# Shifting where the matmul operands begin in on-chip memory: activations to 0, weights to 64 modulo 256 bytes

## The chip, the cores and the metric

One core of a Trainium2 chip runs one program. The metric is its time on the device in microseconds, median of several runs; each comparison is made on the same chip. TensorE multiplies, VectorE, ScalarE and GpSimd work beside it, and SyncE issues nearly all DMA transfers.

## The reference

One inference step of a two-layer streaming encoder, over 512 new frames of one stream (the prompt) and 16 new frames of each of 8 running streams (the sample), 640 columns of 1024 features in all. Cut to what matters:

```python
def swiglu_ffn(h, g, w_in, w_out):
    a, b = jnp.split(rms_norm(h, g) @ w_in, 2, axis=-1)
    return h + (jax.nn.silu(a) * b) @ w_out

def conv_module(h, hist, ...):
    a, gate = jnp.split(rms_norm(h, g) @ w_pw1 + b_pw1, 2, axis=-1)
    full = jnp.concatenate([hist, a * jax.nn.sigmoid(gate)], axis=1)
    y = depthwise_conv(full, w_dw) + b_dw                    # width 31, causal
    return h + silu(layer_norm(y, ln_g, ln_b)) @ w_pw2 + b_pw2, full[:, -30:]

# layer 0: h = conv_module(h); h = swiglu_ffn(h)
# then   : k, v = split(rms_norm(h, norm_kv) @ w_kv)
# layer 1: q = rms_norm(h, norm_attn) @ w_q; h += band_attention(q, k, v, rel_bias) @ w_o
#          h = swiglu_ffn(h)
# end    : y = rms_norm(h, norm_final)
```

The width is D = 1024, the FFN's hidden width F = 2816 (22 tiles of 128), 16 heads of 64. Everything is float32.

## The kernel before, in words

Features lie on the 128 partitions, frames along the free dimension. The 640 columns are held as two groups, group 0 of 256 columns and group 1 of 384 (`GR`). So a matmul of a weight tile moves either 256 or 384 columns.

**Three products for one.** Precision is kept by splitting every operand into a rounded part and a rest. `wsplit` (L119) loads up to 2048 columns of weights into `raw` (1 MB), ScalarE writes the rounded part `whi` (L141) and VectorE or GpSimd the rest `wlo` (L145); with gains folded in these are L133 and L134. Each of the three tags has two buffers in the pool `wp`. `xsplit` (L149) does the same for activations, at L150 and L151. The normalised activations of a group are kept as `xh` and `xl` (`new_xs`, L153), here called `xs`; the FFN's hidden activations as a pair `hid`. `mm3` (L158) then issues, for each tile of the contraction, three matmuls into one accumulator:

```python
for i, ((wh, wl), (xh, xl)) in enumerate(zip(wts, xs)):
    nc.tensor.matmul(ps, wh, xh, start=(i == 0), stop=False)          # L161
    nc.tensor.matmul(ps, wl, xh, start=False, stop=False)             # L162
    nc.tensor.matmul(ps, wh, xl, start=False, stop=(i == last))       # L163
```

The second argument is stationary (loaded into the array), the third moves through it. In almost all uses the weights are stationary. `proj_v` (L660) is the other way round: there `xs` is stationary and the weights move, 256 columns at a time.

**The stages**, in order: the pointwise layers and the convolution (`pw1`, `conv`, `pw2`; VectorE does most of the convolution at L425) interleaved, by a written plan, with the first part of FFN 0; the rest of FFN 0; attention with its projections (`proj_kq` L638, `proj_v`, `proj_o`, and the heads); FFN 1; the final norm.

**The FFN** (`ffn`, L309) takes the 22 hidden tiles in chunks. For each hidden tile, `ffn_in` (L259) multiplies 2 halves x 8 tiles of the contraction x 3 products, 48 matmuls a group, moving `xs`. Then `ffn_out` (L293) takes the chunk's hidden tiles as contraction and produces 8 output tiles, moving `hid`. In layer 0 group 0 runs alone for 18 hidden tiles in chunks of 6, then both groups for a chunk of 4, then group 1 alone for 18 in chunks of 6. In layer 1 both groups run together, group 1 ahead of group 0 for each hidden tile, in chunks of 9, 9 and 4; an output tile of a 9-chunk is 27 matmuls a group, and group 1 and group 0 alternate. With a chunk of 4, an output tile is 12 matmuls, and the 8 tiles of one group run ahead of the 8 of the other.

**Where buffers begin.** A pool hands out addresses in each partition one after the other, each tile rounded up to 32 bytes. The pool `cst` comes first: the residual stream `h`, small constants, the tile `i4` (L342), then the four tiles `xh`, `xl` of both groups, some more, and as its last tile `t256s` (L579). Then come the weight pool `wp`, and behind it all the other pools, which follow its end. `XPAD` lengthens `i4` and so moves `xs` and all that is behind it; `WPAD` lengthens `t256s` and so moves the weights and all that is behind them. `OPAD` and `HPAD` pad single tiles further on.

Of the kernel before, what the change touches and what calls it, by code (L numbers as in the profile page):

```python
# [54 lines left out]
SSQ = 'avavavav'  # L55
SCUT = 8
CB, QB, KB = 5, 1, 1
XPAD, WPAD, OPAD, HPAD = 24, 8, 16, 16
OG = (0, 1)
BO = "a0 s0 a1 s1 b0 b1 t0 p0 c0 t1 c1"  # L60
BL = "a0 s0 a1 s1 t0 b0 b1 c0 t1 c1 p0"
# [912 lines left out]
```

## Time and profile before

| | |
|---|---|
| time before, median of 3 runs | 1578.71 us (1578.55 to 1582.74) |
| the profiled execution's own time | 1581.78 us |
| its span, first to last instruction | 1580.0 us, mean granted clock 0.983 |
| TensorE matmul busy | 1506.5 us (95%), 10998 matmuls |
| VectorE busy | 970.0 us (61%) |
| ScalarE busy | 604.6 us (38%) |
| GpSimd busy | 398.1 us (25%) |
| DMA | 199.98 MB, mean 127 GB/s |

Lines such as L161 are lines of the kernel; a group of instructions is named by line, engine, operation, and out <- in by the program's tile names with buffer numbers left out (`mm<-xh,whi`: an accumulator from `xh` and `whi`). PE is the matmul, PEld the load of its stationary operand, which overlaps other matmuls. The shown duration of a matmul (280 ns and more) is its passage through the pipeline; a stream of them starts one every 113 to 177 ns, which is read from the start times of the timeline.

### The profile page before, as it was taken

How to read it: one execution, taken by the hardware profiler on the slowest of the kernel's cores; microseconds unless marked ns; L12 is line 12 of the kernel's file. 1: busy time of each engine (PE TensorE's matmuls, PEld its weight loads, DVE VectorE, ACT ScalarE, POOL GpSimd, SP SyncE). 2: the span in 40 equal slices, each digit the busy share in tenths (PEclk: the TensorE clock that was granted, in tenths of full speed). 3: DMA queues.
4: the chain of work that ended last, by engine and by line, in shares of the span. 5: the costliest groups of instructions: out<-in, count | busy, mean ns of one | idle time of the engine just before them, and what ended most of it. 6: DMA issues, size and time to landing. Idle time of an engine off the chain costs nothing.

```text
span 1580.0 us, 26820 instructions
## 1 busy us (share of the span) xinstructions
PE 1506.5 (95%) x10998; PEld 1435.8 (91%) x10998; DVE 970.0 (61%) x1781; ACT 604.6 (38%) x1064; POOL 398.1 (25%) x368
## 2 busy tenths in 40 slices
PE   5988998989999999999999999998999999999997
PEld 5868898889999999999987798886999999999997
DVE  5995999978544555456776668576644334433345
ACT  4544454535433323235654345443422112221222
POOL 6864568867501000004221111011200000000001
PEclk9999999999999999999999999998999999999998
DMA  7884345444412333433655554550221231212311
GB/s 238 237 227 136 123 128 163 138 161 142 150 56 81 121 124 117 147 114 118 234 179 168 177 186 155 162 182 28 81 73 48 66 121 58 77 46 76 107 54 67
DMA packets 58700, 199.98 MB, mean 127 GB/s; under 512 B 10193, under 2 KB 22737, under 8 KB 45777
## 3 DMA queue, kind: packets, MB, share of 16 engines
q1 hardware_dynamic: 58288, 197.96, 38.9%
q8 instruction: 86, 1.41, 0.4%
q10 hardware_dynamic: 288, 0.31, 0.1%
q14 instruction: 38, 0.30, 0.1%
HBM read 187.02 MB, written 11.22 MB: 125 GB/s over the span
## 4 chain that ended last, share of the span: by engine, by line
PE 74%; DVE 15%; DMA 3%; ACT 3%; issue 2%; POOL 2%; SPq 0%; POOLq 0%; ACTq 0%; DVEq 0%
PE mm L161 22%; PE mm L163 22%; PE mm L162 22%; DVE w L425 5%; DVE wlo L145 4%; PE w L780 1%; DMA x<-sc 1%; DVE xl L151 1%; PE am L765 1%; PE am L748 1%; PE am L811 1%; ACT whi L141 1%; DVE hid L151 1%; DMA raw<-in_w_pw 1%; PE w L724 1%
## 5 line engine op out<-in xcount | busy, mean ns | idle before, releaser
L162 PE MATMUL mm<-xh,wlo 128*128 128x256 f32 (+1 forms) x2048 | 636.3, 312 | 14.3 <-DVE wlo L145 13.7
L161 PE MATMUL mm<-xh,whi 128*128 128x256 f32 (+1 forms) x2048 | 632.7, 312 | 7.8 <-ACT xh L150 3.6
L163 PE MATMUL mm<-xl,whi 128*128 128x256 f32 (+1 forms) x2048 | 632.6, 311 | 1.0 <-DVE xl L151 0.9
L162 PEld LDWEIGHTS mm<-xh,wlo 128*128 128x128 f32 x2048 | 390.3, 191 | 17.5 <-DVE wlo L145 16.5
L161 PEld LDWEIGHTS mm<-xh,whi 128*128 128x128 f32 x2048 | 388.2, 191 | 13.0 <-ACT xh L150 6.6
L163 PEld LDWEIGHTS mm<-xl,whi 128*128 128x128 f32 x2048 | 388.6, 190 | 3.5 <-DVE xl L151 2.4
L141 ACT ACTIVATE whi<-raw 128x2048 fp32r<-128x2048 f32 (+3 forms) x140 | 235.0, 1682 | 333.7 <-PE mm L163 278.4
L145 DVE TENSOR_TENSOR wlo<-raw,whi 128x2048 fp32r<-128x2048 f32 (+6 forms) x140 | 262.1, 1874 | 77.8 <-ACT whi L141 77.2
L162 PE MATMUL mm<-hid,wlo 128*128 128x384 f32 (+1 forms) x704 | 216.4, 308 | 6.6 <-DVE wlo L145 6.6
L163 PE MATMUL mm<-hid,whi 128*128 128x384 f32 (+1 forms) x704 | 214.2, 307 | 0.1
L161 PE MATMUL mm<-hid,whi 128*128 128x384 f32 (+1 forms) x704 | 212.8, 307 | 0.0
L145 POOL TENSOR_TENSOR wlo<-raw,whi 128x1536 fp32r<-128x1536 f32 (+3 forms) x50 | 145.3, 2910 | 72.1 <-ACT whi L141 71.5
L280 DVE TENSOR_TENSOR t<-mm,bc 128x384 f32<-128x384 f32 x66 | 33.9, 513 | 188.7 <-PE mm L163 188.7
L162 PEld LDWEIGHTS mm<-hid,wlo 128*128 128x128 f32 x704 | 132.1, 188 | 8.0 <-DVE wlo L145 8.0
L163 PEld LDWEIGHTS mm<-hid,whi 128*128 128x128 f32 x704 | 132.1, 188 | 0.5 <-DVE hid L151 0.3
L161 PEld LDWEIGHTS mm<-hid,whi 128*128 128x128 f32 x704 | 131.2, 188 | 0.2
L218 POOL TENSOR_TENSOR rst<-rst,mhalf 128x2 f32<-128x2 f32 (+1 forms) x7 | 5.9, 849 | 452.5 <-DVE rst L214 452.5
L291 DVE TENSOR_TENSOR h<-mm,h 128x384 f32<-128x384 f32 (+1 forms) x112 | 53.9, 486 | 104.4 <-PE mm L163 104.3
L425 DVE SCALAR_TENSOR_TENSOR w<-gp,dwv,w 128x384 f32<-128x384 f32 x180 | 103.9, 611 | 0.8
L279 ACT ACTIVATE t<-t 128x384 f32<-128x384 f32 x66 | 32.3, 489 | 159.2 <-DVE t L278 159.2
L150 ACT ACTIVATE hid<-t 128x384 fp32r<-128x384 f32 (+1 forms) x88 | 40.5, 461 | 116.9 <-DVE t L281 83.4
L184 POOL TENSOR_TENSOR acc<-sq,sq 128x384 f32<-128x384 f32 (+1 forms) x9 | 9.3, 1028 | 265.0 <-ACT sq L168 264.9
(154 smaller groups left out, 1896.5 us busy)
## 6 DMA issues: line engine op xcount, KB each, us to landing
raw<-in_w_in SPq DMA_DIRECT2D x62, 1024.0 KB
raw<-in_w_pw SPq DMA_DIRECT2D x22, 1024.0 KB
raw<-in_w_out SPq DMA_DIRECT2D x24, 768.0 KB
cache<-in_ck SPq DMA_DIRECT2D x32, 512.0 KB
cache<-in_cv SPq DMA_DIRECT2D x32, 512.0 KB
raw<-in_w_out SPq DMA_DIRECT2D x16, 576.0 KB
raw<-in_w_kq SPq DMA_DIRECT2D x8, 1024.0 KB
x<-sc SPq DMA_DIRECT2D x16, 368.0 KB
```

The lines of the kernel that those rows point to most:

```text
L141: nc.scalar.activation(out=hi[:, a:b], in_=raw[:, a:b], func=AF.Copy)
L145: eng.tensor_tensor(out=lo[:, a:b], in0=raw[:, a:b], in1=hi[:, a:b].bitcast(F32), op=ALU.subtract)
L150: nc.scalar.activation(out=hi, in_=src, func=AF.Copy)
L151: nc.vector.tensor_tensor(out=lo, in0=src, in1=hi.bitcast(F32), op=ALU.subtract)
L161: nc.tensor.matmul(ps, wh, xh, start=(i == 0), stop=False)
L162: nc.tensor.matmul(ps, wl, xh, start=False, stop=False)
L163: nc.tensor.matmul(ps, wh, xl, start=False, stop=(i == last))
L279: nc.scalar.activation(out=s[:, :n], in_=s[:, :n], func=AF.Silu)
L280: nc.vector.tensor_tensor(out=t[:, :n], in0=ps[1], in1=bc, op=ALU.mult)
L291: nc.vector.tensor_tensor(out=hp(g, m), in0=pt[:, :n], in1=hp(g, m), op=ALU.add)
L425: nc.vector.scalar_tensor_tensor(out=dst, in0=src, scalar=wj, in1=dst, op0=ALU.mult, op1=ALU.add)
L724: nc.tensor.matmul(ps, QQ[:, q], KK[:, 0:n], start=True, stop=False)
```

## The change

One line of constants:

```diff
-XPAD, WPAD, OPAD, HPAD = 24, 8, 16, 16
+XPAD, WPAD, OPAD, HPAD = 0, 40, 16, 16
```

The pads count float32 elements. `i4` shrinks from 56 to 32 elements, 96 bytes, so everything behind it in `cst` begins 96 bytes earlier. `t256s` grows from 16 to 48 elements (its pad is now 160 bytes long), 128 bytes, so `wp` and all pools behind it begin 128 - 96 = 32 bytes later. Start addresses modulo 256, from the pools' addresses:

| tiles | before | after |
|---|---|---|
| `h`, `vec`; `ident` | 128; 0 | 128; 0 |
| `xh`, `xl`, both groups | 96 | 0 |
| `raw`, `whi`, `wlo`, both buffers | 32 | 64 |
| `hid`, all of them | 224 | 0 |
| `KK`, `KL`, `QQ`, `ohi`, `olo` (attention, but for the last pair of heads, where `ohi`, `olo` lie at 32 before and 64 after) | 224 | 0 |
| scores `S` | 32 | 64 |
| moving minus stationary, weights stationary, `xs` moving | 64 | 192 |
| the same, `hid` moving | 192 | 192 |
| the same, `proj_v` (`xs` stationary, weights moving) | 192 | 64 |

Pieces of these tiles begin at multiples of 512 bytes from their start, so each matmul's operands have the same remainders. No instruction is added, removed or moved: the five engines' orders, and the waits in them, are the same in both programs.

## The prediction

> **What bounds the kernel now.** I read the page first, then the busy time by stretch, then the chain of work that ended last in three stretches, and last the timeline at the borders between groups of matmuls. The page's span and its row of busy engines:
>
> ```profile
> span 1580.0 us, 26820 instructions
> PE 1506.5 (95%) x10998; PEld 1435.8 (91%) x10998; DVE 970.0 (61%) x1781; ACT 604.6 (38%) x1064; POOL 398.1 (25%) x368
> ```
>
> The busy time by stretch (length, then each engine's busy us and instructions, granted clock, DMA share, GB/s):
>
> ```profile
> 244.00:391.00 147.00, 131.20 (x1039) 127.64 (x1038) 132.42 (x193) 69.24 (x89) 114.28 (x58) 0.95 0.47 153
> ...
> 511.00:738.00 227.00, 226.12 (x1305) 225.80 (x1303) 120.02 (x149) 79.03 (x98) 7.78 (x9) 1.00 0.37 122
> 738.00:1103.00 365.00, 354.86 (x3052) 304.68 (x3052) 245.88 (x699) 169.82 (x448) 68.67 (x115) 0.99 0.50 164
> ...
> 1125.00:1233.00 108.00, 108.00 (x748) 108.00 (x748) 46.08 (x73) 27.25 (x40) 0.00 (x0) 1.00 0.20 66
> ```
>
> The chain by line, in the three stretches 154 to 391, 391 to 738 and 1103 to 1571:
>
> ```profile
> by line: DVE w L425 32.9%; DVE wlo L145 21.4%; DVE hid L151 5.4%; issue 5.1%; PE mm L162 4.8%; PE mm L163 4.5%; PE mm L161 4.3%; DVE xl L151 3.2%; ACT whi L141 2.8%; DMA raw<-in_w_pw 2.1%; ACT cvt L404 1.8%; DVE h L291 1.7%; DVE t L276 1.6%
> ...
> by line: PE mm L163 31.8%; PE mm L162 31.6%; PE mm L161 31.5%; DVE xl L151 1.4%; ACT whi L133 1.4%; ACT whi L141 0.5%; DVE wlo L145 0.4%; PE w L205 0.3%; PE w L193 0.3%; ACT xh L150 0.2%; issue 0.2%; DVE h L291 0.1%; ACT sq L168 0.1%; ACT n
> ...
> by line: PE mm L163 32.8%; PE mm L162 32.6%; PE mm L161 32.6%; POOL h L886 0.9%; issue 0.4%; PE w L205 0.4%; PE w L193 0.3%; ACT b L876 0.1%; DVE h L694 0.1%
> ```
>
> The reader is to see two kernels in one. From 391 to 738 and from 1103 to 1571 us TensorE alone sets the end: the three matmul lines of `mm3` are 95% and 98% of the chain, and in 1125 to 1233 PE is busy 108.00 of 108.00 us at clock 1.00. There, a nanosecond per matmul goes straight into the span. From 154 to 391 VectorE ends the waits (convolution L425, weight split L145), and those PE lines are 4.8 + 4.5 + 4.3 = 13.6% of the chain.
>
> So the question is what one matmul costs from start to start. The timeline has it at the borders of unbroken runs (start, us, engine, line, operands, tile, form, count):
>
> ```profile
> 482.69 0.28 PE L161 MATMUL mm<-hid,whi 128*128 128x256 f32 x1
> ...
> 493.99 0.34 PE L161 MATMUL mm<-hid,whi 128*128 128x384 f32 x1
> ...
> 510.95 0.34 PE L161 MATMUL mm<-xh,whi 128*128 128x384 f32 x1
> ...
> 636.74 0.34 PE L161 MATMUL mm<-hid,whi 128*128 128x384 f32 x1
> ...
> 661.89 0.34 PE L161 MATMUL mm<-xh,whi 128*128 128x384 f32 x1
> ...
> 1213.35 0.28 PE L161 MATMUL mm<-xh,whi 128*128 128x256 f32 x1
> ...
> 1219.00 0.34 PE L161 MATMUL mm<-xh,whi 128*128 128x384 f32 x1
> ...
> 1227.32 0.28 PE L161 MATMUL mm<-xh,whi 128*128 128x256 f32 x1
> ...
> 1232.98 0.34 PE L161 MATMUL mm<-hid,whi 128*128 128x384 f32 x1
> ...
> 1237.75 0.28 PE L161 MATMUL mm<-hid,whi 128*128 128x256 f32 x1
> ...
> 1240.83 0.33 PE L161 MATMUL mm<-hid,whi 128*128 128x384 f32 x1
> ...
> 1245.51 0.28 PE L161 MATMUL mm<-hid,whi 128*128 128x256 f32 x1
> ...
> 1248.57 0.33 PE L161 MATMUL mm<-hid,whi 128*128 128x384 f32 x1
> ...
> 1538.70 0.34 PE L161 MATMUL mm<-hid,whi 128*128 128x384 f32 x1
> ...
> 1555.66 0.28 PE L161 MATMUL mm<-hid,whi 128*128 128x256 f32 x1
> ```
>
> The counts between borders are the code's loops. Moving `xs` (48 a block: 2 halves x 8 k x 3 products), 256 wide: (1219.00 - 1213.35) / 48 = 117.7 ns; 384 wide: 8.32 / 48 = 173.3 ns. Moving `hid` in the second FFN (27 a tile: 9 k x 3), 256 wide: (1248.57 - 1245.51) / 27 = 113.3 ns; 384 wide: 4.68 / 27 = 173.3 ns. So the same line, shape and clock takes 4.4 ns less with `hid`, 3.7%. But `hid` has slower paces too. After the `xs` block at 117.7 its first 384-wide tile takes 4.77 / 27 = 176.7 ns (1232.98 to 1237.75); then it recovers. In the four-tile chunk of the first FFN (96 matmuls each) it runs at 11.30 / 96 = 117.7 ns and 16.96 / 96 = 176.7 ns, and the last chunk's 384-wide part repeats the 176.7 (1538.70 to 1555.66). Alone at 384 wide, from 636.74 to 661.89 (144), it runs at 174.7 ns.
>
> What separates the operands is where they begin. Mod 256, the weights lie at 32, `xs` at 96 and `hid` at 224: moving minus stationary is 64 for `xs` and 192 for `hid`. A third pair tests this without `hid`: the V projection moves the weights over stationary `xs`, a distance of 32 - 96, again 192. Its first group, and one later (24 matmuls each):
>
> ```profile
> 744.02 0.28 PE L161 MATMUL mm<-whi,xh 128*128 128x256 f32 x1
> ...
> 746.76 0.28 PE L161 MATMUL mm<-whi,xh 128*128 128x256 f32 x1
> ...
> 759.24 0.28 PE L161 MATMUL mm<-whi,xh 128*128 128x256 f32 x1
> ...
> 762.06 0.28 PE L161 MATMUL mm<-whi,xh 128*128 128x256 f32 x1
> ```
>
> 2.74 / 24 = 114.2 ns, near the 113.3, and 2.82 / 24 = 117.5 ns: both paces again. My reading: distance 64 allows one stable pace at 256 wide, 117.7, and the best one at 384; distance 192 allows 113.3 and 117.7 at 256 wide and three paces at 384, and which one holds depends on the pace at which a run enters. 113.3 at 256 and 173.3 at 384 hand over to each other; 117.7 hands 176.7 to the next 384-wide run.
>
> **The change part by part.** The order of instructions is the same on all five engines, so only addresses can act. After it `xs` and `hid` lie at 0 and the weights at 64: moving minus stationary becomes 192 for `xs`, stays 192 for `hid`, and becomes 64 for the V projection.
>
> (1) Second FFN, 1103 to 1571: 22 hidden tiles x 48 = 1056 `xs` matmuls of 256, at 113.3 instead of 117.7: -4.6 us. Its 1056 of 384 stay at 173.3, as `hid` shows in the same alternation. The bad entries go: 2 x 27 x (176.7 - 173.3) = -0.2; and the closing chunk, entered at 113.3, gives 96 x 3.4 + 96 x 4.4 = -0.75.
>
> (2) Four-tile chunk of the first FFN, 391 to 511: 4 x 48 x 4.4 = -0.85, and its `hid`, entered at 113.3, 96 x 4.4 + 96 x 3.4 = -0.75.
>
> (3) Wide part of the first FFN, 511 to 738: 864 `xs` matmuls of 384 and 432 of `hid`. Ends: all at 173.3, 432 x 1.4 = -0.6; all at 176.7, 864 x 3.4 + 432 x 2.0 = +3.8. I take 174.7, what `hid` alone at this width shows nearest: 864 x 1.4 = +1.2.
>
> (4) Attention, 738 to 1103, PE-led but with waits after which the pace is drawn anew. K and Q: 384 of 256 wide, between 0 and -1.7, half: -0.85; 384 of 384 wide, between 0 and +1.3 (176.7), at 0.7 each: +0.3. V: 480 matmuls lose their 113.3 share, between 0 and 480 x 4.4 = +2.1, half: +1.05. Sum +0.5.
>
> (5) Before 391: 8 x 48 matmuls of 256 in the first pointwise layer, 8 x 24 in the second, 18 x 48 in the first FFN: at most 1440 x 4.4 = -6.3. But in 154 to 391 the chain gives PE 13.6%; VectorE's splits would simply be waited for longer. 1440 x 4.4 x 0.136 = -0.9, less the share of entries at 117.7: -0.6.
>
> (6) Everything else moves by 32 bytes or not at all. VectorE, by form:
>
> ```profile
> L291 DVE TENSOR_TENSOR h<-mm,h 128x384 f32<-128x384 f32 x56 | 30.8, 555 | 62.2 <-PE mm L163 62.1
> ...
> L151 DVE TENSOR_TENSOR hid<-t,hid 128x384 fp32r<-128x384 f32 x44 | 24.4, 555 | 13.0 <-ACT hid L150 12.4 <-issue 0.6
> ...
> L748 PE MATMUL am<-ident,S 128*128 128x128 f32 x160 | 24.4, 274 | 0.2
> ```
>
> `h` lies at 128 and `hid` at 224 mod 256, and both forms take 555 ns: VectorE gets 0. The transposes pair `ident`, which stays at 0, with `S`, which goes from 32 to 64; 160 of them by up to 4.4 ns either way is +-0.7: I take 0, since nothing shows a sign. DMA into weights shifted by 32 bytes is bounded by the same stretch: at a DMA share of 0.20 PE waits for nothing, so 0 there.
>
> Sum: -4.6 - 0.2 - 0.75 - 0.85 - 0.75 + 1.2 + 0.5 - 0.6 = -6.05. The profiled execution took 1581.8 us (span 1580.0, 1.8 around it), 3.1 over the median of 1578.7: by it 1575.7, by the median 1572.7.
>
> **A rule against it.** By these rows, the distance between two streams that TensorE reads costs 4.4 ns a matmul. The Trainium skill (SBUF — State Buffer, "Who interferes with whom") says that TensorE reads moving data and weights through two independent ports, and that it never waits on anyone; by that rule no address matters and the sum is 0. The trace disagrees: 117.7 against 113.3 ns.
>
> **The rivals.** A: paces mixed. Each entry falls to 113.3 or 117.7 as in V's two groups, and the second FFN does not settle. Half of (1) and (2), -3.6; (3) and (4) as above, +1.7; 1056 wide `xs` matmuls at 174.7, +1.5; half of (5), -0.3. Sum -0.7: 1578.0, no change that can be told. For it: V, and 176.7 seen at three entries. Against: after one bad tile the second FFN's `hid` runs settled from 1240.83 on.
>
> B: the 4.4 ns have a cause other than the distance, one that stays with `xs` wherever it lies: 0, 1578.7. By the rule of the page above this is what happens. Against: V, where neither operand is `hid`.
>
> C, slower: the bad pair locks. A 256-wide run at 117.7 hands over 176.7, and gets 117.7 back: so it stands from 482.69 to 510.95. Place: second FFN. Price: 1056 `xs` x 3.4 = +3.6, and 14 `hid` pairs x 27 x (4.4 + 3.4) = +2.9; four-tile chunk 192 x 3.4 = +0.65; (3) at its worst, +3.8; (4) +2.4. Sum +13.35: 1592.1. It decides when a 176.7 run hands over 117.7; at 1237.75 it handed over about 113.3.
>
> **How the numbers follow.** A measurement can tell about 0.3% from no change, 4.7 us. Forecast 0.60, A 0.22, B 0.08, C 0.10. The forecast with (3) at +3.8 is -3.45 and counts as no change: I give that 0.05. So faster 0.55, same 0.35, slower 0.10. Range: the low end takes (3) at -0.6, (4) at -1.4 and (5) at -2.5 (two fifths of its bound), sum -11.65: 1567.1. The high end takes in A, B and a mild C, in which (1) and (2) still give half, -3.6 and -0.3, but wide runs and V come at their dearest, +3.8 + 1.5 + 2.1: +3.5, 1582.2.
>
> **What would show it.** In the new profile, runs of 48 `xs` matmuls of 256 in the second FFN should last 5.44 us, not 5.65, next to 8.32 for the wide ones. V's groups of 24 should all take 2.82. The stretch 511 to 738 shows (3): 4.16 us a group of 24 is 173.3, 4.19 is 174.7, 4.24 is 176.7. Wide `xs` blocks at 8.48 beside 5.65 would be C; 5.65 beside 8.32 everywhere, B. If the end moves while these stay, my reading is wrong.

## The result, and the profile after

The changed kernel takes 1570.52 us (median of 5 runs, 1568.41 to 1573.84), the kernel before 1578.71 in the same session: a ratio of 0.9942, interval 0.9924 to 0.9961. That is 8.2 us less; 6.05 were forecast, and 1572.7 us. The profiled execution took 1573.84 us.

The page's span and its row of busy engines:

```profile
span 1572.1 us, 26820 instructions
PE 1497.4 (95%) x10998; PEld 1426.5 (91%) x10998; DVE 970.1 (62%) x1781; ACT 605.0 (38%) x1064; POOL 396.8 (25%) x368
```

TensorE lost 9.1 us of busy time with the same 10998 matmuls, and the other engines lost nothing that matters (VectorE 970.0 and 970.1). The busy time by stretch (length, then each engine's busy us and instructions, granted clock, DMA share, GB/s), and the chain by line in 154 to 391 and in 1103 to 1563:

```profile
511.00:738.00 227.00, 225.70 (x1316) 225.41 (x1315) 121.86 (x155) 80.48 (x105) 11.62 (x14) 1.00 0.38 122
738.00:1103.00 365.00, 354.21 (x3031) 303.80 (x3030) 244.31 (x695) 168.71 (x442) 63.84 (x111) 0.98 0.50 163
...
1125.00:1233.00 108.00, 108.00 (x758) 108.00 (x757) 46.52 (x72) 28.01 (x41) 0.00 (x0) 1.00 0.20 65
```

```profile
by line: DVE w L425 33.1%; DVE wlo L145 21.4%; DVE hid L151 5.3%; issue 4.9%; PE mm L162 4.5%; PE mm L163 4.3%; PE mm L161 4.1%; DVE xl L151 3.2%; ACT whi L141 2.8%; DMA raw<-in_w_pw 2.1%; ACT cvt L404 1.8%; DVE h L291 1.7%; DVE t L276 1.6%
...
by line: PE mm L163 32.7%; PE mm L162 32.7%; PE mm L161 32.7%; POOL h L886 0.9%; issue 0.4%; PE w L205 0.4%; PE w L193 0.3%; ACT b L876 0.1%
```

The bounds are the old ones: PE is still busy 108.00 of 108.00 us at clock 1.00 in the second FFN, but 758 matmuls now fall into the time of 748. So there the matmuls follow each other faster. The timeline at the borders between runs (start, us, engine, line, operands, tile, form):

```profile
479.91 0.28 PE L161 MATMUL mm<-hid,whi 128*128 128x256 f32 x1
...
490.79 0.33 PE L161 MATMUL mm<-hid,whi 128*128 128x384 f32 x1
...
507.43 0.34 PE L161 MATMUL mm<-xh,whi 128*128 128x384 f32 x1
...
633.17 0.34 PE L161 MATMUL mm<-hid,whi 128*128 128x384 f32 x1
...
658.13 0.51 PE L161 MATMUL mm<-xh,whi 128*128 128x384 f32 x2
...
740.01 0.28 PE L161 MATMUL mm<-whi,xh 128*128 128x256 f32 x1
...
742.73 0.28 PE L161 MATMUL mm<-whi,xh 128*128 128x256 f32 x1
...
755.23 0.28 PE L161 MATMUL mm<-whi,xh 128*128 128x256 f32 x1
...
758.06 0.28 PE L161 MATMUL mm<-whi,xh 128*128 128x256 f32 x1
...
1127.39 0.28 PE L161 MATMUL mm<-xh,whi 128*128 128x256 f32 x1
...
1132.86 0.33 PE L161 MATMUL mm<-xh,whi 128*128 128x384 f32 x1
...
1141.17 0.28 PE L161 MATMUL mm<-xh,whi 128*128 128x256 f32 x1
...
1146.62 0.33 PE L161 MATMUL mm<-xh,whi 128*128 128x384 f32 x1
...
1229.17 0.33 PE L161 MATMUL mm<-hid,whi 128*128 128x384 f32 x1
...
1233.85 0.28 PE L161 MATMUL mm<-hid,whi 128*128 128x256 f32 x1
...
1236.91 0.33 PE L161 MATMUL mm<-hid,whi 128*128 128x384 f32 x1
```

In the second FFN an `xs` block of 48 at 256 wide takes 5.45 us (1141.17 to 1146.62), 113.5 ns a matmul where it was 117.7, beside 8.31 for the wide block. `hid` is entered without a bad tile: 4.68 / 27 = 173.3 and 3.06 / 27 = 113.3 ns. In the first FFN the four-tile chunk's `hid` takes 10.88 / 96 = 113.3 and 16.64 / 96 = 173.3 ns, where it took 117.7 and 176.7. Alone at 384 wide (633.17 to 658.13) it takes 24.96 / 144 = 173.3 ns, where it took 174.7. The V projection now has both paces too: 2.72 / 24 = 113.3 and, later, 2.83 / 24 = 117.9.

The same matmuls taken as borders in both programs give the change of every stretch, in us (stretches named by the old program's times; the differences are worked out from the matmuls' starts in the two traces; the last column is a second profile of the changed kernel, experiment e9 below):

| stretch | predicted | measured | again (e9) |
|---|---|---|---|
| before 391 | -0.6 | -2.1 | -4.6 |
| 391 to 482, first FFN, four tiles, `xs` | -0.85 | -0.50 | -0.64 |
| 482 to 511, its `hid` | -0.75 | -0.75 | -0.75 |
| 511 to 738, wide part | +1.2 | -0.30 | -0.29 |
| 738 to 1103, attention | +0.5 | +1.7 | -0.95 |
| 1103 to 1125 | 0 | -0.06 | -0.06 |
| 1125 to 1539, second FFN | -4.8 | -4.61 | -4.61 |
| 1539 to 1568, its closing chunk | -0.75 | -0.71 | -0.71 |

The second FFN and the two chunks of `hid` repeat to the hundredth; the stretches with waits do not. The traces of e3 and e7 below contain the changed kernel as well, with matmuls added behind its end, and have the same -4.61 in the second FFN.

### The profile page after: what moved, and what is told of

Same layout as the page of the kernel before. It is cut to its first block, busy times and chain, and to the rows that moved or that the text cites. A ratio compares the mean times of both kernels' runs of the same rounds, so it can differ in the third digit from the quotient of the medians.

```text
span 1572.1 us, 26820 instructions
## 1 busy us (share of the span) xinstructions
PE 1497.4 (95%) x10998; PEld 1426.5 (91%) x10998; DVE 970.1 (62%) x1781; ACT 605.0 (38%) x1064; POOL 396.8 (25%) x368
## 4 chain that ended last, share of the span: by engine, by line
PE 74%; DVE 15%; POOL 3%; issue 3%; ACT 2%; DMA 2%; SPq 0%; POOLq 0%; ACTq 0%; DVEq 0%
PE mm L161 22%; PE mm L162 22%; PE mm L163 22%; DVE w L425 5%; DVE wlo L145 4%; PE w L780 1%; DVE xl L151 1%; DMA x<-sc 1%; PE am L765 1%; POOL y L405 1%; PE am L748 1%; ACT whi L141 1%; PE am L811 1%; PE mm L457 1%; DVE hid L151 1%
```

## The experiments

The theories: **D**, the prediction's, the distance of the two start addresses mod 256 sets the pace. **M**, the moving operand's own start does. **G**, whether both starts are multiples of 64 does. Then, where several paces are possible: **L**, a run holds the pace that it is handed, and **N**, its rival, that it doesn't. **P** came last: whether a wide run hands over a slow pace depends on how many matmuls it has. The "good pair" below is 113.3 ns at 256 wide with 173.3 at 384, the "bad pair" 117.8 with 176.7. Edits are shown against the kernel before for e1, e2 and e4, against e5 for e8, and otherwise against the changed kernel; ratios are always to the kernel before.

**e1: the distances of the change at other positions.** The weights and all that is behind them move by 128 bytes: `xs` stays at 96, the weights go to 160 and `hid` to 96, so that the distances are 192, 192 and, for V, 64, as in the changed kernel. `x4` is cut a little to make room.

```diff
-XPAD, WPAD, OPAD, HPAD = 24, 8, 16, 16
+XPAD, WPAD, OPAD, HPAD = 24, 40, 16, 16
-        x4 = cp.tile([P, 4, GSW], F32, tag="x4", name=nm("x4"))
+        x4 = cp.tile([P, 4, GSW - 4], F32, tag="x4", name=nm("x4"))
```

> Only the weights move (and all that lies behind them): weights at 160, xs stays at 96, hid at 96, mod 256. Theory D, the distance moving minus stationary sets the pace: it is 192 for xs and hid, as in the change, so the second FFN's blocks of 48 xs matmuls of 256 last 5.44 us, the wide blocks 8.32, and the ratio is 0.994 to 0.996. Theory M, the moving operand's own start sets it and 96 is the start that never reaches 113.3: xs blocks stay at 5.65 us, hid (now at 96 too) goes from 3.06 to 3.18 us a tile of 27, and the ratio is 1.000 to 1.003. Theory G, the gain is of transfers, VectorE or ScalarE through 64-byte alignment: starts behind the weights stay 32 off a multiple of 64, so nothing changes, ratio 1.000, with hid as before.

Measured: 1580.52 us, ratio 1.0009, interval 0.9997 to 1.0022: no change. The timeline shows why:

```profile
637.86 0.34 PE L161 MATMUL mm<-hid,whi 128*128 128x384 f32 x1
...
663.30 0.52 PE L161 MATMUL mm<-xh,whi 128*128 128x384 f32 x2
...
1139.98 0.34 PE L161 MATMUL mm<-xh,whi 128*128 128x384 f32 x1
...
1148.46 0.28 PE L161 MATMUL mm<-xh,whi 128*128 128x256 f32 x1
...
1154.12 0.34 PE L161 MATMUL mm<-xh,whi 128*128 128x384 f32 x1
...
1238.92 0.34 PE L161 MATMUL mm<-hid,whi 128*128 128x384 f32 x1
...
1243.69 0.28 PE L161 MATMUL mm<-hid,whi 128*128 128x256 f32 x1
...
1246.77 0.33 PE L161 MATMUL mm<-hid,whi 128*128 128x384 f32 x1
```

The wide blocks take 8.48 / 48 = 176.7 ns and the others 5.66 / 48 = 117.9: the pair that rival C of the prediction names, held for the whole first chunk of the second FFN. `hid` enters with a tile at 4.77 / 27 = 176.7, recovers (3.08 / 27 = 114.1), and the rest of the FFN has the good pair: -1.69 us instead of -4.61. From 511 to 738 every wide matmul takes 176.7 (25.44 / 144 in the first two rows): +3.7, next to the upper end of +3.8 that the prediction gave, and attention takes 2.3 us more than before in this profile. So D's time was missed, and the time that M and G forecast was met: distance alone does not bring the gain. Yet M falls, since `xs` at its old start of 96 does reach 113.3 in the later chunks, and G, since the weights lie 32 off a multiple of 64 there.

**e2: the activations move alone.** `xs` to 0, `hid` to 128, weights to 192: all starts are multiples of 64, and the distance of `xs` is 64 as before.

```diff
-XPAD, WPAD, OPAD, HPAD = 24, 8, 16, 16
+XPAD, WPAD, OPAD, HPAD = 0, 8, 16, 16
```

> Only the activations' pad goes, so xs is at 0, weights at 192, hid at 128 mod 256: moving minus stationary is 64 for xs, as before the change, and 192 for hid. Theory D: xs blocks of 48 at 256 wide stay at 5.65 us, wide ones at 8.32, ratio 0.999 to 1.002. Theory M: xs at 0 runs as in the change, 5.44 us, and the ratio is 0.994 to 0.996. Theory G: weights and all behind them now begin at multiples of 64, as in the change, so the gain is there, 0.994 to 0.996, without a shorter xs block.

Measured: 1578.36 us, ratio 0.9990, interval 0.9978 to 1.0002. In the second FFN:

```profile
1133.23 0.34 PE L161 MATMUL mm<-xh,whi 128*128 128x384 f32 x1
...
1141.55 0.28 PE L161 MATMUL mm<-xh,whi 128*128 128x256 f32 x1
...
1147.20 0.34 PE L161 MATMUL mm<-xh,whi 128*128 128x384 f32 x1
```

8.32 / 48 = 173.3 and 5.65 / 48 = 117.7 ns, the old pair; the stretches 511 to 738 and 1125 to 1539 differ from before by 0.00 us. D's forecast is met, M's and G's are not. `xs` lies where the changed kernel has it, everything is aligned to 64, and nothing is gained.

**e3: the distance measured by itself.** The changed kernel with 64 groups of matmuls added behind its end, in the manner of `mm3`: each moves 48 of 256, 24 of 384, 48 of 256 and 24 of 384 columns, for 8 x 8 start addresses. The whole time says nothing here (2879.39 us).

```diff
...
+    for xi, xa in enumerate("abcdefgh"):
+        for wi, wa in enumerate("abcdefgh"):
+            pt = lq.tile([P, 4, 512], F32, tag="lad", name="x" + xa + "w" + wa)
+            for part, (n, reps) in enumerate(((256, 2), (384, 1), (256, 2), (384, 1))):
+                for _ in range(reps):
+                    mm3(pt[:, part, :n],
+                        [(WH[:, 8 * wi + k * P:8 * wi + (k + 1) * P],
...
+            nc.scalar.activation(out=sink, in_=pt[:, :, 0], func=AF.Copy)
```

> The changed kernel with 64 groups of 144 matmuls behind its end, one for each pair of starts mod 256 in steps of 32 (moving and stationary operand in eight positions each): 48 of 256 wide, 24 of 384, 48 of 256, 24 of 384, with nothing else running and a wait between groups; its time is about 1.3 ms longer and tells nothing by itself. Theory D: the pace depends on the difference alone; at 64 all eight positions give 117.7 at 256 wide and 173.3 at 384, at 192 mostly 113.3 and 173.3. Theory M: the pace depends on the moving start alone; start 96 gives 117.7 whatever the weights' start is.

The names give the starts: a is 64, then 32 more a letter, g is 0. In the order of time: `xawc` (192), `xawg` (64) and `xgwa` (192, the starts of `xs` and weights in the changed kernel). Each time the second, third and fourth part begin:

```profile
1623.08 0.34 PE L161 MATMUL xawc<-XH,WH 128*128 128x384 f32 x1
...
1627.28 0.28 PE L161 MATMUL xawc<-XH,WH 128*128 128x256 f32 x1
...
1632.93 0.34 PE L161 MATMUL xawc<-XH,WH 128*128 128x384 f32 x1
...
1704.69 0.34 PE L161 MATMUL xawg<-XH,WH 128*128 128x384 f32 x1
...
1708.85 0.28 PE L161 MATMUL xawg<-XH,WH 128*128 128x256 f32 x1
...
1714.51 0.34 PE L161 MATMUL xawg<-XH,WH 128*128 128x384 f32 x1
...
2557.74 0.33 PE L161 MATMUL xgwa<-XH,WH 128*128 128x384 f32 x1
...
2561.89 0.28 PE L161 MATMUL xgwa<-XH,WH 128*128 128x256 f32 x1
...
2567.34 0.33 PE L161 MATMUL xgwa<-XH,WH 128*128 128x384 f32 x1
```

With 24 and 48 matmuls between the rows: `xawc` 175.0 and 117.7 ns, `xawg` 173.3 and 117.9, `xgwa` 172.9 and 113.5 (rounded as the rows are). All 64, worked out in the same way from the third and fourth part (48 and 23 steps):

| distance mod 256 | ns at 256 wide | ns at 384 wide |
|---|---|---|
| 0 | 119.7 (8 of 8) | 173.6 |
| 32 | 116.7 (7), 117.8 (1) | 173.3 (4), 176.7 (4) |
| 64 | 117.8 (8) | 173.3 |
| 96 | 119.7 to 120.0 (8) | 176.8 |
| 128 | 118.7 (8) | 175.8 |
| 160 | 118.7 (8) | 176.5 |
| 192 | 113.4 (5), 117.8 (3) | 173.2 (5), 174.8 (3) |
| 224 | 118.3 (8) | 173.3 |

At six of the eight distances all eight pairs of starts agree within 0.3 ns. At 32 and at 192 they split between two or three pairs of paces, so there the distance sets which paces are possible and something else picks one. In these streams D holds in the form that the prediction gave it: distance 192 is the only one of the eight that reaches 113.3, and it has more than one stable pace.

**e4: one group at each distance.** `xs` of group 0 at distance 192, of group 1 at 64, by a gap ahead of group 1's tiles.

```diff
-XPAD, WPAD, OPAD, HPAD = 24, 8, 16, 16
+XPAD, WPAD, OPAD, HPAD = 0, 8, 16, 16
+        if g == 1 and not gap:
+            gap.append(cst.tile([P, 32], F32, name="gap", tag="gap"))
+            nc.gpsimd.memset(gap[0][:, 0:1], 0.0)
```

> A gap of 128 bytes ahead of group 1's activations: xs of group 0 at 0, of group 1 at 128, weights at 64, hid at 0 mod 256. Moving minus stationary is 192 for group 0 (256 wide), 64 for group 1 (384 wide), 192 for hid. Both theories: wide xs matmuls at 173.3 ns everywhere, none at 174.7 or 176.7. Theory N, distance 192 by itself gives 113.3 at 256 wide: 5.44 us for each block of 48 in the second FFN, ratio 0.993 to 0.995. Theory L, at distance 192 the pace is the one that the matmuls before hand over, and a wide run at distance 64 hands over 117.7, as xs did to hid at 482.69 of the profile before: 5.65 us a block, ratio 0.999 to 1.002.

Measured: 1576.96 us, ratio 0.9991, interval 0.9978 to 1.0003. In the second FFN (line 165 is the former 161):

```profile
1131.37 0.34 PE L165 MATMUL mm<-xh,whi 128*128 128x384 f32 x1
...
1139.69 0.28 PE L165 MATMUL mm<-xh,whi 128*128 128x256 f32 x1
...
1145.34 0.34 PE L165 MATMUL mm<-xh,whi 128*128 128x384 f32 x1
```

The wide block at distance 64 takes 8.32 / 48 = 173.3, and the narrow one takes 5.65 / 48 = 117.7 although it lies at 192: so in the whole second FFN (0.00 us against before). L's forecast is met and N's is not: a block at 192 does not fall to 113.3 by itself.

**e5 and e6: two more pairs of positions at distance 192**, `xs` at 32 and weights at 96 (`XPAD, WPAD = 8, 40`), then 64 and 128 (`16, 40`).

```diff
-XPAD, WPAD, OPAD, HPAD = 0, 40, 16, 16
+XPAD, WPAD, OPAD, HPAD = 8, 40, 16, 16
```

> The changed kernel with everything from xs on 32 bytes further: xs at 32, weights at 96, hid at 32 mod 256, all distances as in the change. Theory N: as the change, ratio 0.993 to 0.996. Theory L: the runs of matmuls between two waits hold either 113.3 with 173.3 or 117.7 with 176.7, and which pair a program falls into is not set by the distance; the ratio lies anywhere between 0.993 (all in the first) and 1.008 (all in the second), and the profile shows whole stretches of the one or the other.

> As the run before, 32 bytes further again: xs at 64, weights at 128, hid at 64, distances as in the change. Theory N: ratio 0.993 to 0.996. Theory L: anywhere between 0.993 and 1.008, by which pair holds in the second FFN (about 8 us between the two) and in the wide part of the first (about 4 us).

Measured: e5 1574.73 us, ratio 0.9975 (0.9959 to 0.9991); e6 1572.89, ratio 0.9971 (0.9956 to 0.9985). Both lie between e1 and the change. In both the second FFN gains 1.69 us as in e1, while 511 to 738 has the good pace (-0.29 and -0.30). In e5 the first chunk's `hid` begins so:

```profile
1234.88 0.34 PE L161 MATMUL mm<-hid,whi 128*128 128x384 f32 x1
...
1239.65 0.28 PE L161 MATMUL mm<-hid,whi 128*128 128x256 f32 x1
```

4.77 / 27 = 176.7, and good from then on: the bad pair held until a run of 27, as in e1.

**e7: what a run at distance 192 does after different entries.** Behind the changed kernel: for eight start addresses, blocks of 48 (256, 384, 256, 384 wide) at 192 that begin after a wait (`ea`), straight behind 24 matmuls of 256 at distance 64 (`eb`), or behind 24 of 384 at 64 (`ec`). Then streams with V's step of 1024 bytes between weight pieces, at 64 and at 192. Then streams whose distance to their own stationary operand is 192 and to the next one 64, and the reverse.

```diff
+        for entry in range(3):
+            pt = lad("e" + L[entry] + "x" + L[xi])
+            if entry:
+                n = (0, 256, 384)[entry]
+                stream(pt[:, 3, :n], n, xi, xi - 2)
+            for part, n in enumerate((256, 384, 256, 384)):
+                for _ in range(2):
+                    stream(pt[:, part, :n], n, xi, xi + 2)
...
```

> The changed kernel with three sets of matmul streams behind its end, its time tells nothing. Set 1, distance 192 in eight positions, entered after a wait, straight behind 24 matmuls of 256 at distance 64, and straight behind 24 of 384 at distance 64: theory N gives 113.3 at 256 wide in all; theory L gives both paces, and more 117.7 behind matmuls at distance 64. Set 2, 256 wide with the stationary pieces 1024 bytes apart as in the V projection, at distances 64 and 192: by distance alone 64 gives 117.7 in all positions and 192 mostly 113.3; if the step matters, 64 gives 113.3 too, as it did in the V projection of the changed kernel. Set 3, each matmul at distance 192 of its own stationary operand and 64 of the next one, and the other way round: if the pace comes of the load of the next operand, which runs beside a matmul, the first gives 117.7 and the second mostly 113.3; if it comes of the matmul's own operand, the reverse.

At the changed kernel's own starts, after a wait, and behind 24 of 256 at distance 64:

```profile
2134.84 0.34 PE L161 MATMUL eaxg<-XH,WH 128*128 128x384 f32 x1
...
2143.32 0.28 PE L161 MATMUL eaxg<-XH,WH 128*128 128x256 f32 x1
...
2148.98 0.34 PE L161 MATMUL eaxg<-XH,WH 128*128 128x384 f32 x1
...
2160.88 0.28 PE L161 MATMUL ebxg<-XH,WH 128*128 128x256 f32 x1
...
2166.32 0.33 PE L161 MATMUL ebxg<-XH,WH 128*128 128x384 f32 x1
...
2174.63 0.28 PE L161 MATMUL ebxg<-XH,WH 128*128 128x256 f32 x1
```

8.48 / 48 = 176.7 and 5.66 / 48 = 117.9 after the wait; 5.44 / 48 = 113.3 and 8.31 / 48 = 173.1 behind the 24. So the same instructions at the same addresses have two self-sustaining pairs. After a wait 6 of 8 took the bad one and kept it for 192 matmuls; behind 24 at distance 64, of either width, all 16 took the good one. That is against L as I had it, by which a run at distance 64 hands on 117.7: in e4 it did, here it did not. The pace of the run ahead is therefore not all that is handed over. V's step alone makes no difference: 117.8 at distance 64 in 8 of 8, 113.3 at 192 in 7 of 8. So the 113.3 of V's first group in the changed kernel (740.01 to 742.73, at distance 64) is explained neither by the distance nor by the step; streams entered behind other matmuls, as V's are, were not tried at this distance. The last set tells nothing: 116.7 and 176.6 in all 16, whichever of the two distances was the own one.

**e8: three matmuls more.** P comes from counts: at 176.7, runs of 48 and 96 (the closing chunk before the change) hand on 117.8, runs of 27 (e1, e5, and the kernel before) hand on about 113.3. Three matmuls that compute nothing used are added behind group 1's block of the third hidden tile, in e5's kernel, so that this one run has 51.

```diff
+            if wsrc is w_in1 and j == 2 and g == 1:
+                pt = mmt()
+                mm3(pt[:, :n], [(wh[:, 0:P], wl[:, 0:P])], xk(xs[g], range(1)))
```

> The kernel with xs at 32 and weights at 96 (the run that held 176.7 and 117.7 through the first chunk of the second FFN, two fifths of the saving), and three more matmuls of 384 (their product goes nowhere) behind the wide block of the third hidden tile: 51 instead of 48. Theory P: at distance 192 a wide run at 176.7 hands 117.7 on if its count is a multiple of six, as 48 and 96 did, and 113.3 at 27; 51 is three off a multiple of six as 27 is, so from there on the blocks take 5.44 and 8.32 us, and the stretch of the second FFN gets about 2.3 us shorter than in that run (seven of its nine hidden tiles at 0.38 less, less 0.5 for the three matmuls, and the two 27-tiles kept): ratio 0.994 to 0.997. Theory N, this position itself gives the slow pair: no change from that run but 0.5 us more, ratio 0.997 to 0.999.

Measured: 1573.51 us, ratio 0.9953 (0.9937 to 0.9968), e5 0.9975. The two intervals overlap, so the timeline has to decide:

```profile
1133.27 0.34 PE L161 MATMUL mm<-xh,whi 128*128 128x384 f32 x1
...
1141.75 0.34 PE L161 MATMUL mm<-xh,whi 128*128 128x384 f32 x1
...
1142.28 0.28 PE L161 MATMUL mm<-xh,whi 128*128 128x256 f32 x1
...
1147.74 0.33 PE L161 MATMUL mm<-xh,whi 128*128 128x384 f32 x1
```

48 matmuls in 8.48 us (176.7), the three more until 1142.28, then a 256-wide block in 5.46 (113.8), and 173.2 from there on: the stretch 1125 to 1539 is 3.7 us shorter than before, the 0.5 us of the three included, where e5 was 1.69 shorter: 2.0 net, where P gave about 2.3. Three matmuls more take the FFN out of the bad pair, some 90 us before its first `hid` would have. P's forecast is met, on one run; six matmuls more, which by P's rule (a multiple of six hands 117.8 on) should change nothing, were not tried, so any other break in the rhythm remains a rival.

**e9: the changed kernel again**, without an edit, to see which stretches are settled by the program.

> The changed kernel itself once more, on another chip. If the pair that holds is drawn anew in each execution, its profile shows other stretches at 117.7 and 176.7 than before, and its times spread over some 8 us; if the program settles it, the second FFN recovers at its second hidden tile again, and the ratio is 0.993 to 0.996. The attention stage, 1.7 us longer in the first profile, shows whether that repeats.

Measured: 1570.14 us, ratio 0.9937 (0.9918 to 0.9956). Its stretches are the last column of the table above.

## Why the prediction was right, and where it was not

**The mechanism, right where the weights are stationary.** The reading that the distance of the two starts mod 256 sets which paces exist, that 64 has 117.7 at 256 wide and 192 has 113.3 as well, is what e2 and e3 show. For V it is not enough: at 64, six of its twenty groups stay under 114 ns in their unbroken steps (three in e9), and at 192, before, nine did. The rule of the Trainium skill (SBUF — State Buffer, "Who interferes with whom"), two independent read ports and an engine that never waits on anyone, stood for rival B: by it the sum was 0. What the prediction drew from it, that no address matters, does not hold here: 113.4 to 120.0 ns for the same stream of matmuls by its addresses alone, with VectorE, GpSimd and DMA at rest (e3).

**(1) The second FFN, -4.8, measured -4.61.** 1056 matmuls were counted; the block at 1127.39 is the first whole one at the good pace, and 21 hidden tiles x 48 x 4.4 ns = 4.43, with 0.2 for the bad entries that are gone. So rival A, in which the FFN does not settle, is out for this program. But that it would settle was luck in part: at three other positions with the same distances it did so only at the first `hid` (e1, e5, e6: -1.69), which is rival C's mechanism at its place, "a 176.7 run hands over 117.7". The chance of 0.10 that C had was too low for positions at large. What the prediction took as the point of decision, the 27-run at 1237.75 that recovered, was no evidence for runs of 48: in e5 they kept the bad pair, and in e8 one of 51 left it.

**(2) The four-tile chunk, -0.85 and -0.75, measured -0.50 and -0.75.** Right, but for a part of the `xs` blocks.

**(3) The wide part, +1.2, measured -0.30: mis-sized, with the wrong sign.** I took 174.7 for wide runs at 192, from one `hid` run in the kernel before. Here they run at 173.3 (the 288 from 507.43 take 49.92 us, behind a block at 173.3). e3 has 174.7 as the wide partner of 117.8; so that row described another entry, not the distance. The upper end, +3.8, was right: e1 reaches +3.7. The lower, -0.6, took all `hid` from 174.7 to 173.3; the `hid` matmuls behind waits did not follow, and -0.30 came.

**(4) Attention, +0.5, measured +1.7 and, again, -0.95.** The step "V would always take 2.82" failed: V at distance 64 still has groups at 113.3 (why stays open), and its mean is 116.4 (117.0 in e9) where it was 115.5: 480 x 0.9 = 0.4 us (0.7 in e9) of the 1.05 forecast. Nor are K and Q what was taken: their 256-wide ones go from 117.7 to 116.0 and their 384-wide ones from 173.6 to 174.0. These terms sum to 480 x 0.9 - 384 x 1.7 + 384 x 0.4 = -0.07 us; the other +1.8 of the first profile is in waits. It did not come again in e9, but the same stretch has +2.2 in e3's trace and +0.3 in e7's, which run the same instructions there. So it scatters by more than was forecast, and is not explained further.

**(5) Before 391, -0.6, measured -2.1 and -4.6.** Multiplying the saving by PE's share of the chain, 13.6%, was wrong: that share is no price for runs between two waits. From 245 to 391 alone it is -2.6 (e9 -3.1); the seven experiments with `xs` of group 0 at distance 192 (e1, e3 to e8) have -1.8 to -3.3 there, and e2, at 64, -0.02. So it goes with the distance. The 576 `xs` matmuls there went from 117.8 to 115.3, 1.4 us; the rest, 1.2 us in the first profile, is in shorter waits between them, half of it in one (3.84 to 3.25 us), and why these got shorter was not found.

**(6) The rest, 0.** VectorE's busy time is the same, 970.1 us. What the transposes gained or lost can't be told from the waits of attention.

The errors of (3) and (5), -1.5 each, and of (4), +1.2, leave -1.8; (1) and (2) give 0.5 of that back. The stretches sum to -7.3 and the span fell by 7.9, so the forecast is near because (1) and the `hid` of (2), -6.1 together, carry it, and because the errors of the other parts cancel in part, which is luck.

What stays open: what a run hands over besides its pace (e4 against e7); why V reaches 113.3 at distance 64; why the entry at 1127 recovers in the changed kernel and not in e1, e5 and e6; whether the distance to the own or to the next stationary operand counts.

The single steps give a hint on the third. Ahead of 1127.39 stand 16 wide matmuls, four small ones of L205, then 32 wide ones at 176.7, whose steps repeat every six matmuls. The first step of the 32 takes 260 ns in all four traces of the changed kernel's starts (the profile after, e3, e7, e9), and 264 or 265 in e1, e5, e6 and e8. Where it is 260, the next block begins with steps of about 118, 124 and 118 ns and recovers, as behind the 51 matmuls of e8. So the place in the cycle of six at which a run ends may be what it hands over; no run varies that by itself.

## What to carry to other kernels

Where TensorE alone sets the end, read the time from start to start of a matmul for each pair of operands, before counting anything else; two operands of the same form with different paces point to their start addresses. A pace seen once may be one of several that hold themselves, so look at what hands over to what, and at how many matmuls the run before has. Changing addresses is judged by the timeline of the kernel itself, since the same distance gave ratios from 0.9942 to 1.0009 at four positions.

## What the runs showed of the hardware

- The difference of the start addresses of moving and stationary operand, mod 256 bytes, sets which paces a matmul takes in unbroken streams of this form: 113.4 to 120.0 ns at 256 columns, 173.2 to 176.8 at 384 (table in e3). The V projection is an exception: at 64 some of its groups run at 113.3, where e3 and e7 have 117.8.
- At difference 192 two pairs, 113.3 with 173.3 and 117.8 with 176.7, hold themselves over hundreds of matmuls in the same code (e1, e7), and a third, 117.8 with 174.8, shows in e3.
- Leaving the bad pair went with the number of matmuls: 384-wide runs of 27 or 51 left it (e1, e5, e8), runs of 48 or 96 did not. Three matmuls more took 0.5 us and saved 2.5 in e8. Where other matmuls stand shortly ahead, the number alone does not tell: 32 wide matmuls left it in the changed kernel (1127.39) and kept it in e1, e5 and e6.
- After a wait, 6 of 8 streams entered the bad pair; behind 24 matmuls at difference 64 none of 16 did (e7).
